# GpSimd instead of VectorE takes the remainder of every third weight block in a two-layer encoder

## The chip, the cores and the metric

One core of a Trainium2 chip runs the kernel. The metric is the device time of one execution in microseconds (us); the median of several runs is compared. Engines are named as in the profile: PE is TensorE (PEld its weight loads), DVE is VectorE, ACT is ScalarE, POOL is GpSimd, SP is the queue that issues most transfers.

## What is computed

A two-layer encoder on 256 tokens of 2048 numbers, all in float32:

```
x = x + neighbourhood_attention(rms_norm(x, na_norm))       # 16 heads of 128, learned bias
x = x + square(relu(rms_norm(x, ffn0_norm) @ ffn0_w1)) @ ffn0_w2     # 2048 -> 8192 -> 2048
x = x + dilated_attention(rms_norm(x, dil_norm))            # 3 groups of 8 heads
x = x + square(relu(rms_norm(x, ffn1_norm) @ ffn1_w1)) @ ffn1_w2
out = rms_norm(x, final_norm)
```

Nearly all of the work is products of the 256 tokens with weights. Each operand is cut into a rounded part and what is left of it, and a product is the sum of rounded x rounded, rounded x rest and rest x rounded.

## The kernel before

The weights are cut into 400 blocks of 512 x 512 numbers (1 MB), and the program is a list of 400 steps, one for each block; block i is used in step i. In the neighbourhood attention, steps 0 to 47, each of four groups of heads has twelve steps: four for q, four for k, four for v. Steps 48 to 63 are its output projection, then come feed-forward 0 (64 to 191), the dilated attention (192 to 271) and feed-forward 1 (272 to 399).

A step has four quarters of products on PE. Between them stand the small tasks of attention (scores, transposes, outputs). Nothing is scheduled by a tool: each engine takes its instructions in the order in which the loop at the end of the program writes them.

A block passes four hands. SP loads it into the tile w (three buffers). ACT then writes the rounded part wh of one half of the block (line 104), and DVE writes the rest, wl = w - wh (line 105); PE reads both. Each half has tiles of its own, and there are four buffers of wh and of wl, so two blocks' worth. In step i the first half of block i + 2 is cut behind quarter 1, the second half behind quarter 3; only then is block i + 5 loaded (lines 745 to 760), into the buffer of w that block i + 2 leaves. A half is named here (block, half), so (24, second) is the second half of block 24.

Two more things stand in these queues around the change. For each group of heads SP loads a bias, two transfers behind each of the steps 12c + 4 to 12c + 7 and thus behind the loads of the blocks 12c + 9 to 12c + 12 (`load_bias`, line 332; c is 0 to 3). DVE masks it after step 12c + 8 (`mask_bias`, line 338), adds it to the scores (line 368), takes the maximum (line 404), waits for ACT's exponentials (line 407) and scales (line 411). In the last step of q and of k, ACT copies half of the sums (line 144), DVE adds the other half (z, line 146) and scales z (line 348).

Of the kernel before, what the change touches and what calls it, by code (L numbers as in the profile page):

```python
# [8 lines left out]
F32 = mybir.dt.float32  # L9
F32R = mybir.dt.float32r  # L10
AF = mybir.ActivationFunctionType
ALU = mybir.AluOpType
AX = mybir.AxisListType

P = 128
# [11 lines left out]


class Step:
    """One weight block [4 x 128, 512], the products that it takes part in (in four  # L30
    quarters) and the work that goes with them: tasks have a part on the tensor engine
    after a quarter, evac reads the finished sums, post follows."""

    def __init__(self, src, quarters):
        self.src = src
# [7 lines left out]
def tile_encoder(ctx: ExitStack, tc: tile.TileContext, ins, out):  # L43
    nc = tc.nc
# [13 lines left out]
    x = const.tile([P, 2, D], F32, name="x")  # L58
# [9 lines left out]

    x_in = ins["x"].rearrange("(t p) d -> p t d", p=P)

# [1 line left out]
    steps = []  # L72

    def load(i):
# [11 lines left out]
    def prep(i, u):  # L86
        if i >= len(steps):
            return
        s = steps[i]
        hi = hlpool.tile([P, 2, 512], F32R, name="wh", tag="wh")  # L90
        lo = hlpool.tile([P, 2, 512], F32R, name="wl", tag="wl")
        part = s.w[:, 2 * u:2 * u + 2, :]
        if i:
            split(hi, lo, part)
        else:
            for a in range(2):
                split(hi[:, a], lo[:, a], part[:, a])
        s.hi[u], s.lo[u] = hi, lo
# [6 lines left out]
        nc.vector.tensor_tensor(out=dst_lo, in0=src, in1=dst_hi.bitcast(F32), op=ALU.subtract)  # L105

    def three(o, left, right, start, stop):
        """o += left.T @ right, both in two parts; the product of the two rests is below float32."""
        nc.tensor.matmul(o, left[0], right[0], start=start, stop=False)  # L109
        nc.tensor.matmul(o, left[0], right[1], start=False, stop=False)  # L110
        nc.tensor.matmul(o, left[1], right[0], start=False, stop=stop)  # L111

# [1 line left out]
    def gemm_cols(w, col, xT, nk, done):  # L114
        acc = {}
        made = []
# [39 lines left out]
        nc.tensor.matmul(o, xh, wl, start=False, stop=False)  # L156
        nc.tensor.matmul(o, xl, wh, start=False, stop=stop)  # L157

# [1 line left out]
    def gemm_rows(w, col, xT, ks, acc, first_k, last_k, apart=False):  # L160
        made = []
        for k in ks:
# [10 lines left out]
            made.append(s)  # L173
        return made

# [1 line left out]
    class Norm:  # L177
        def __init__(self, n, perm):
            self.n, self.perm = n, perm
# [68 lines left out]
            nc.vector.tensor_copy(self.r, self.r_ps[:, 0, 0:4].rearrange("p (t u) -> p t u", u=2)[:, :, 0])  # L248

    def rsqrt_mean(ss):  # L250
        """1 / sqrt(mean + eps) of the sums of squares: a root, its reciprocal and one step of Newton's on it."""
        a = small.tile([P, 2], F32, name="ms", tag="ms", bufs=2)
        nc.vector.tensor_reduce(out=a, in_=ss, op=ALU.add, axis=AX.X)
        nc.vector.tensor_scalar(out=a, in0=a, scalar1=1.0 / D, scalar2=EPS, op0=ALU.mult, op1=ALU.add)
        r = small.tile([P, 2], F32, name="rstd", tag="rstd", bufs=2)
        nc.scalar.sqrt(r, a)
        nc.vector.reciprocal(r, r)
        u = small.tile([P, 2], F32, name="ru", tag="ru", bufs=2)
        nc.vector.tensor_tensor(out=u, in0=r, in1=r, op=ALU.mult)
        nc.vector.tensor_tensor(out=u, in0=u, in1=a, op=ALU.mult)  # L260
        nc.vector.tensor_scalar(out=u, in0=u, scalar1=-0.5, scalar2=1.5, op0=ALU.mult, op1=ALU.add)
        nc.vector.tensor_tensor(out=r, in0=r, in1=u, op=ALU.mult)
        return r

    # x += rows; at the end of a sublayer the next norm is begun
    def add_rows(made, col_block, acc, norm, chunk_done):
        cs = slice(col_block * 512, (col_block + 1) * 512)
        if norm is not None and norm() in fin and col_block == NB - 1:
# [19 lines left out]
        later.append((i, pe, post, quarter))  # L288

    def pending_norm(get):  # L290
        """Hooks behind the steps that finish x's column blocks."""
        def chunk_done(step, c):
            i = steps.index(step)
            for half in range(2):
                at(i + 1, lambda half=half: get().transposes(c, half), lambda half=half: get().parts(c, half),
                   quarter=1 + half)
            if c == NB - 1:
                at(i, None, lambda: get().rstd())
                at(i + 2, lambda: get().rows(), lambda: get().rows_out())
                if get().perm:  # L300
                    at(i + 3, lambda: get().cols(), lambda: get().cols_out())
        return chunk_done

# [1 line left out]
    norms = [Norm(0, False), None, None, None]  # L305

    n0 = norms[0]
# [11 lines left out]
        return hi, lo  # L319

    class NaHeads:
        """Four heads: their q, k, v, bias and the steps from scores to outputs."""

        def __init__(self, c):
            self.c = c

        # bias[c + 64 e, h, o, 63 - c'] is for the query (2 t + e, c) and the key (o - 2 + 2 t, c')
        def load_bias(self, h):
            if h == 0:
                self.bias = big.tile([P, 4, 6, GRID_W], F32, name="bias", tag="big")  # L330
# [68 lines left out]
            split(t[:, h, 0, :], t[:, h, 1, :], self.o[:, 0, :])  # L399

    def softmax(p):
        """p [P, 2, n]: each row of n becomes its softmax."""
        m = small.tile([P, 2], F32, name="m", tag="m")
        nc.vector.tensor_reduce(out=m, in_=p, op=ALU.max, axis=AX.X, negate=True)
        z = small.tile([P, 2], F32, name="sum", tag="sum")
        for tb in range(2):
            nc.scalar.activation(p[:, tb, :], p[:, tb, :], AF.Exp, bias=m[:, tb:tb + 1],
                                 accum_out=z[:, tb:tb + 1])
        nc.vector.reciprocal(z, z)
        for tb in range(2):  # L410
            nc.vector.tensor_scalar(out=p[:, tb, :], in0=p[:, tb, :], scalar1=z[:, tb:tb + 1], scalar2=None,
                                    op0=ALU.mult)
# [4 lines left out]
    for c in range(4):  # L417
# [5 lines left out]
        i = steps.index(made[0])  # L423
# [5 lines left out]
        i = steps.index(made[0])  # L429
# [3 lines left out]
               lambda H=H, h=h, task=task: getattr(H, task + "_post")(h))  # L433

    def rows_apart(pair, xT, acc, finish):
        """The last two blocks of a sum of four: the first half of the tokens through both, then the second."""
        for tb, s in enumerate(pair):
            def quarter(s, n, tb=tb):
                for a in (n % 2 * 2, n % 2 * 2 + 1):
                    products(acc[tb], pair[n // 2], xT[2 + n // 2], a, slice(tb * P, (tb + 1) * P),  # L440
                             False, n == 3 and a == 3)
            s.quarters = quarter
            s.evac.append(lambda tb=tb: finish(tb, acc))
# [16 lines left out]
    out_rows(ins["na_wo"], na_oT, 4, lambda: norms[1], begin_norm(1, False),  # L460
             [(c, k) for c in range(3) for k in range(3)] + [(c, 3) for c in range(3)] + [(3, k) for k in range(4)])

# [1 line left out]
    def ffn(norm, w1, w2, next_norm, next_done):  # L464
        for g in range(4):
            hT = [None] * 4
# [14 lines left out]

    ffn(norms[1], ins["ffn0_w1"], ins["ffn0_w2"], lambda: norms[2], begin_norm(2, True))

# [1 line left out]
    n2 = norms[2]  # L485
    dil_oT = [None] * 2
    rope = {}
# [142 lines left out]
    out_rows(ins["dil_wo"], dil_oT, 2, lambda: norms[3], begin_norm(3, False),  # L630
             [(0, 0), (1, 0), (0, 1), (1, 1), (2, 0), (2, 1), (3, 0), (3, 1)])

# [1 line left out]
    class Final:  # L634
        perm = False

# [30 lines left out]
        def finish(self, tb, acc):  # L667
            cs = slice((NB - 1) * 512, D)
            nc.vector.tensor_tensor(out=x[:, tb, cs], in0=x[:, tb, cs], in1=acc[tb], op=ALU.add)
            self.square(NB - 1, tb)  # L670
            ms = small.tile([P, 1], F32, name="fms", tag="fms", bufs=2)
            nc.vector.tensor_scalar(out=ms, in0=self.ss[:, tb, NB - 1:], scalar1=1.0 / D,
                                    scalar2=self.part[:, tb:tb + 1], op0=ALU.mult, op1=ALU.add)
            # -2 / sqrt(ms): a root, its reciprocal and one step of Newton's on it; the gain has the factor -1/2
            r = small.tile([P, 1], F32, name="fr", tag="fr", bufs=2)
            nc.scalar.sqrt(r, ms)
            nc.vector.reciprocal(r, r)
            u = small.tile([P, 1], F32, name="fu", tag="fu", bufs=2)
            nc.vector.scalar_tensor_tensor(out=u, in0=r, scalar=ms, in1=r, op0=ALU.mult, op1=ALU.mult)
            nc.vector.scalar_tensor_tensor(out=r, in0=u, scalar=-3.0, in1=r, op0=ALU.add, op1=ALU.mult)  # L680
            for c in range(NB):
                cs = slice(c * 512, (c + 1) * 512)
                if c == 0:
                    nc.vector.tensor_scalar(out=x[:, tb, cs], in0=x[:, tb, cs], scalar1=r, scalar2=None,
                                            op0=ALU.mult)
                elif c == NB - 1:
                    nc.vector.scalar_tensor_tensor(out=x[:, tb, cs], in0=x[:, tb, cs], scalar=r, in1=self.g[:, cs],
                                                   op0=ALU.mult, op1=ALU.mult)
                else:
                    nc.scalar.activation(x[:, tb, cs], x[:, tb, cs], AF.Copy, scale=r)  # L690
                nc.sync.dma_start(self.o_v[:, tb, cs], x[:, tb, cs])
# [3 lines left out]
    at(len(steps) + 104, None, fin[0].halve)  # L695
    ffn(norms[3], ins["ffn1_w1"], ins["ffn1_w2"], lambda: fin[0], None)

# [1 line left out]
    for i, pe, post, q in later:  # L699
        if pe is None:  # L700
            steps[i].post.append(post)
# [129 lines left out]
```

## Time and profile before

| | us |
|---|---|
| median of 3 runs (2322.45 to 2324.16) | 2322.57 |
| profiled execution, its span | 2320.3 |
| PE busy | 2300.7 |
| DVE busy | 1406.0 |
| ACT busy | 1092.6 |
| POOL busy | 0.7 |

The profiled execution is one more execution; of it the profile gives the span, from the first instruction's start to the last one's end, and no time of its own. The median of the runs is 2.3 us above this span. Engines work side by side, so busy times do not add up; an engine that is busy for nearly all of the span sets its length. Matmuls overlap one another, so a busy PE is not PE at its peak.

### The profile page before, as it was taken

Reading aid. Unit: us, or ns where it says so; the run is one execution under the profiler, and the core shown is the slowest. Engines: PE = TensorE matmul, PEld = TensorE weight load, DVE = VectorE, ACT = ScalarE, POOL = GpSimd, SP = SyncE. Lnnn points to the kernel's source line nnn. Section 1 sums busy time; section 2 is a strip of 40 time slices with the busy share of each in tenths; the row PEclk is TensorE's granted clock in tenths of the full one; section 3 lists DMA queues with packets and bytes.
Section 4 is the critical chain, followed back from the end, with each engine's and each line's share of the span. In section 5 each row is a group of like instructions: output and inputs, shape, how many; then the busy total and the mean of one; then the engine's idle time right before and its main releaser. Section 6 shows DMA issues by size and latency. Waiting matters only on the chain.

```text
span 2320.3 us, 29178 instructions
## 1 busy us (share of the span) xinstructions
PE 2300.7 (99%) x11956; PEld 1963.1 (85%) x11956; DVE 1406.0 (61%) x1635; ACT 1092.6 (47%) x1390; POOL 0.7 (0%) x6
## 2 busy tenths in 40 slices
PE   8999999999999999999999999999999999999998
PEld 7888888888888888888888888888888888888886
DVE  6666765654555555566777667756654654555654
ACT  6444545543443453455444544445543543543443
POOL 0000000000000000000000000000000000000000
PEclk9999999999999999999999999999999999999999
DMA  7555655555555555555555545454555555555553
GB/s 248 169 175 176 191 182 170 182 197 200 182 187 194 185 196 189 193 181 188 189 179 184 177 164 181 164 181 169 191 192 193 182 200 187 189 187 200 200 192 135
DMA packets 73862, 430.36 MB, mean 185 GB/s; under 512 B 19776, under 2 KB 20352, under 8 KB 22528
## 3 DMA queue, kind: packets, MB, share of 16 engines
q1 hardware_dynamic: 73056, 426.80, 54.3%
q8 instruction: 93, 1.52, 0.3%
q10 hardware_dynamic: 672, 1.70, 0.2%
q14 instruction: 41, 0.34, 0.0%
HBM read 426.38 MB, written 2.10 MB: 185 GB/s over the span
## 4 chain that ended last, share of the span: by engine, by line
PE 98%; DMA 1%; DVE 1%; ACT 0%; issue 0%; SPq 0%; ACTq 0%; DVEq 0%
PE acc L134 33%; PE acc L136 17%; PE acc L156 15%; PE acc L155 15%; PE acc L157 15%; PE misc L194 1%; DMA bias<-in_rpb_dram 0%; PE misc L111 0%; PE misc L110 0%; PE misc L109 0%; DVE wl L105 0%; PE misc L593 0%; PE misc L553 0%; PE misc L380 0%; ACT wh L104 0%
## 5 line engine op out<-in xcount | busy, mean ns | idle before, releaser
L105 DVE TENSOR_TENSOR wl<-w,wh 128x1024 fp32r<-128x1024 f32 (+1 forms) x802 | 972.8, 1221 | 735.8 <-ACT wh L104 733.6
L104 ACT CAST wh<-w 128x1024 fp32r<-128x1024 f32 (+1 forms) x802 | 834.9, 1049 | 936.9 <-PE acc L157 460.2
L134 PE MATMUL acc<-xT,wh 128*128 128x512 f32 x3328 | 1178.5, 399 | 0.9 <-ACT wh L104 0.9
L136 PE MATMUL acc<-xT,wl 128*128 128x256 f32 x3328 | 935.0, 281 | 2.3 <-DVE wl L105 2.3
L134 PEld LDWEIGHTS acc<-xT,wh 128*128 128x128 f32 x3328 | 626.4, 188 | 150.4 <-ACT wh L104 1.9
L136 PEld LDWEIGHTS acc<-xT,wl 128*128 128x128 f32 x3328 | 629.8, 189 | 3.7 <-DVE wl L105 3.2
L155 PE MATMUL acc<-wh,hT 128*128 128x512 f32 x1024 | 399.5, 390 | 0.0
L156 PE MATMUL acc<-wl,hT 128*128 128x512 f32 x1024 | 399.0, 390 | 0.0
L157 PE MATMUL acc<-wh,hT 128*128 128x512 f32 x1024 | 398.9, 390 | 0.0
L157 PEld LDWEIGHTS acc<-wh,hT 128*128 128x128 f32 x1024 | 192.3, 188 | 39.9
L155 PEld LDWEIGHTS acc<-wh,hT 128*128 128x128 f32 x1024 | 192.3, 188 | 39.7
L156 PEld LDWEIGHTS acc<-wl,hT 128*128 128x128 f32 x1024 | 192.3, 188 | 39.4
L155 PE MATMUL acc<-wh,xT 128*128 128x512 f32 x320 | 126.7, 396 | 0.0
L156 PE MATMUL acc<-wl,xT 128*128 128x512 f32 x320 | 125.2, 391 | 1.1 <-DVE wl L105 1.1
L157 PE MATMUL acc<-wh,xT 128*128 128x512 f32 x320 | 124.9, 390 | 0.0
L144 ACT COPY b<-acc 128x512 f32<-128x512 f32 x104 | 60.7, 586 | 64.8 <-PE acc L136 59.1
L146 DVE TENSOR_TENSOR z<-acc,b 128x512 f32<-128x512 f32 x104 | 71.5, 691 | 25.8 <-ACT b L144 25.2
L155 PE MATMUL acc<-wh,oT 128*128 128x512 f32 x192 | 76.6, 399 | 0.0
L157 PE MATMUL acc<-wh,oT 128*128 128x512 f32 x192 | 75.0, 391 | 0.0
L156 PE MATMUL acc<-wl,oT 128*128 128x512 f32 x192 | 74.9, 390 | 0.0
L156 PEld LDWEIGHTS acc<-wl,xT 128*128 128x128 f32 x320 | 60.2, 188 | 13.1 <-DVE wl L105 1.8
L157 PEld LDWEIGHTS acc<-wh,xT 128*128 128x128 f32 x320 | 60.1, 188 | 12.5
(123 smaller groups left out, 1044.9 us busy)
## 6 DMA issues: line engine op xcount, KB each, us to landing
w<-in_ffn_w_dram SPq DMA_DIRECT2D x256, 1024.0 KB, 4.8
w<-in_dil_wqkv_dram SPq DMA_DIRECT2D x72, 1024.0 KB, 4.8
w<-in_na_wqkv_dram SPq DMA_DIRECT2D x47, 1024.0 KB, 4.9
w<-in_na_wo_dram SPq DMA_DIRECT2D x16, 1024.0 KB, 4.9
w<-in_dil_wo_dram SPq DMA_DIRECT2D x8, 1024.0 KB, 4.8
bias<-in_rpb_dram SPq DMA_DIRECT2D x32, 96.0 KB, 8.7
out_dram<-x SPq DMA_DIRECT2D x8, 256.0 KB, 2.5
x<-in_x_dram SPq DMA_DIRECT2D x3, 512.0 KB, 7.8
```

Source lines behind the costliest of these rows:

```text
L104: nc.scalar.copy(dst_hi, src)
L105: nc.vector.tensor_tensor(out=dst_lo, in0=src, in1=dst_hi.bitcast(F32), op=ALU.subtract)
L134: nc.tensor.matmul(o, s.hi[a // 2][:, a % 2, cs], xt.rearrange("p h t -> p (h t)"), start=first, stop=False)
L136: nc.tensor.matmul(o[:, :T], s.lo[a // 2][:, a % 2, cs], xt[:, 0, :], start=False, stop=last)
L144: nc.scalar.copy(b, acc[j][:, :, T:])
L146: nc.vector.tensor_tensor(out=z, in0=acc[j][:, :, :T], in1=b, op=ALU.add)
L155: nc.tensor.matmul(o, xh, wh, start=start, stop=False)
L156: nc.tensor.matmul(o, xh, wl, start=False, stop=False)
L157: nc.tensor.matmul(o, xl, wh, start=False, stop=stop)
L194: nc.tensor.transpose(self.tp[:, a, tb * P:(tb + 1) * P], x[:, tb, kt * P:(kt + 1) * P], ident)
```

## The change

In every third block from block 6 on (6, 9, ..., 399: 132 blocks, 264 halves) the subtraction of line 105 is issued on GpSimd. ACT's rounding stays where it was, and so do the tiles, the loads and the products. The other lines of the difference are comments and blank lines that keep the count.

```diff
@@ prep(i, u) @@
         part = s.w[:, 2 * u:2 * u + 2, :]
-        if i:
+        if i > 4 and i % 3 == 0:
+            nc.scalar.copy(hi, part)
+            nc.gpsimd.tensor_tensor(out=lo, in0=part, in1=hi.bitcast(F32), op=ALU.subtract)
+        elif i:
             split(hi, lo, part)
         else:
```

The first place is DVE's queue between the softmax of the first and of the second head in the first group (steps 9 to 11). Before, wl_717 is (11, second), wl_742 and wl_769 are the two halves of block 12, wl_792 is (13, first); p_693 and p_745 are the two heads' scores:

```order
L411 TENSOR_SCALAR p_693<-p_693,sum_698 128x256 x2
L105 TENSOR_TENSOR wl_717<-w_570,wh_716 128x1024
L105 TENSOR_TENSOR wl_742<-w_624,wh_741 128x1024
L368 TENSOR_TENSOR p_745<-misc_734,bias_483 128x256 x2
L404 TENSOR_REDUCE m_748<-p_745 128x2
L409 RECIPROCAL sum_750<-sum_750 128x2
L411 TENSOR_SCALAR p_745<-p_745,sum_750 128x256 x2
L105 TENSOR_TENSOR wl_769<-w_624,wh_768 128x1024
L105 TENSOR_TENSOR wl_792<-w_667,wh_791 128x1024
```

And the same stretch of DVE's queue with the change, where every line number is 3 higher:

```order
L414 TENSOR_SCALAR p_693<-p_693,sum_698 128x256 x2
L108 TENSOR_TENSOR wl_717<-w_570,wh_716 128x1024
L371 TENSOR_TENSOR p_745<-misc_734,bias_483 128x256 x2
L407 TENSOR_REDUCE m_748<-p_745 128x2
L412 RECIPROCAL sum_750<-sum_750 128x2
L414 TENSOR_SCALAR p_745<-p_745,sum_750 128x256 x2
L108 TENSOR_TENSOR wl_792<-w_667,wh_791 128x1024
```

Both halves of block 12 have left DVE: one subtraction fewer stands ahead of the second head's scores, and one fewer behind its scaling. On POOL's queue, empty before at this point, they stand behind those of the blocks 6 and 9, with what each waits for (the first half of a block among other things for its load):

```order
L95 TENSOR_TENSOR wl_457<-w_288,wh_456 128x1024 [waits DVE_49,DMAHW0_49,PE_49,Activation_49]
L95 TENSOR_TENSOR wl_478<-w_288,wh_477 128x1024 [waits DVE_49,PE_49,Activation_49]
L95 TENSOR_TENSOR wl_591<-w_481,wh_590 128x1024 [waits DMAHW3_49,PE_49,Activation_49]
L95 TENSOR_TENSOR wl_621<-w_481,wh_620 128x1024 [waits PE_49,Activation_49]
L95 TENSOR_TENSOR wl_742<-w_624,wh_741 128x1024 [waits DVE_49,DMAHW4_49,Activation_49,Pool_49]
L95 TENSOR_TENSOR wl_769<-w_624,wh_768 128x1024 [waits DVE_49,Activation_49,Pool_49]
```

POOL takes the halves in the order of the blocks and has nothing else to do between them. The second place is SP's queue, where the load of block 12 stands ahead of the last two transfers of the first group's bias. Before:

```order
L332 DMA bias<-in_rpb_dram 64x6x64
L332 DMA bias<-in_rpb_dram 64x6x64 [waits DMAHW3_49]
L81 DMA w<-in_na_wqkv_dram 128x2048 [waits DMAHW4_49,DVE_49]
L332 DMA bias<-in_rpb_dram 64x6x64 [waits DMAHW5_49]
L332 DMA bias<-in_rpb_dram 64x6x64 [waits DMAHW6_49]
```

With the change:

```order
L335 DMA bias<-in_rpb_dram 64x6x64
L335 DMA bias<-in_rpb_dram 64x6x64 [waits DMAHW3_49]
L81 DMA w<-in_na_wqkv_dram 128x2048 [waits DMAHW4_49,Pool_49]
L335 DMA bias<-in_rpb_dram 64x6x64 [waits DMAHW5_49]
L335 DMA bias<-in_rpb_dram 64x6x64 [waits DMAHW6_49]
```

The order is the same, but this load, and the bias behind it, now wait for POOL, since it overwrites the buffer of block 9. It is so in all four groups.

## Rows read from the trace of the kernel before

**Rows 1.** Page, part 1: busy time, share of the span and instructions of each engine.
```profile
PE 2300.7 (99%) x11956; PEld 1963.1 (85%) x11956; DVE 1406.0 (61%) x1635; ACT 1092.6 (47%) x1390; POOL 0.7 (0%) x6
```

**Rows 2.** Busy time by stretch, neighbourhood attention: stretch, length, engines, granted clock, DMA, GB/s.
```profile
50.00:340.00 290.00, 285.27 (x1542) 244.12 (x1541) 195.96 (x270) 141.57 (x221) 0.00 (x0) 1.00 0.57 178
```

**Rows 3.** Timeline, PE at step 12: start, length, [idle before, who ended it].
```profile
85.03 0.50 PE L134 MATMUL acc<-xT,wh 128*128 128x512 f32 x1 [0.35 <-ACT wh L104]
86.29 0.39 PE L136 MATMUL acc<-xT,wl 128*128 128x256 f32 x1 [0.76 <-DVE wl L105]
```

**Rows 4.** Timelines of DVE and ACT ahead of step 12.
```profile
79.17 2.36 DVE L105 TENSOR_TENSOR wl<-w,wh 128x1024 fp32r<-128x1024 f32 x2
81.44 0.75 DVE L368 TENSOR_TENSOR p<-misc,bias 128x256 f32<-128x256 f32 x2
85.01 2.36 DVE L105 TENSOR_TENSOR wl<-w,wh 128x1024 fp32r<-128x1024 f32 x2
...
83.95 1.98 ACT L104 CAST wh<-w 128x1024 fp32r<-128x1024 f32 x2
```

**Rows 5.** Groups by shape: count, busy us, mean ns of one, idle before.
```profile
L105 DVE TENSOR_TENSOR wl<-w,wh 128x1024 fp32r<-128x1024 f32 x798 | 970.2, 1223 | 735.8 <-ACT wh L104 733.6
...
masks.py:199 POOL TENSOR_SCALAR_AFFINE_SELECT ident<-ident 128x128 f32<-128x128 f32 x1 | 0.3, 292 | 0.1
```

**Rows 6.** Timelines of ACT and DVE around the end of step 19.
```profile
135.39 1.05 ACT L104 CAST wh<-w 128x1024 fp32r<-128x1024 f32 x1
...
134.83 1.39 DVE L146 TENSOR_TENSOR z<-acc,b 128x512 f32<-128x512 f32 x2 [0.39 <-ACT b L144]
136.47 1.23 DVE L105 TENSOR_TENSOR wl<-w,wh 128x1024 fp32r<-128x1024 f32 x1 [0.26 <-ACT wh L104]
137.62 1.29 DVE L348 SCALAR_TENSOR_TENSOR z<-z,rbc 128x512 f32<-128x512 f32 x2
...
148.93 1.76 DVE L338 TENSOR_TENSOR bias<-bias,namask 128x1536 f32<-128x1536 f32 x1 [5.41 <-DMA bias<-in_rpb_dram]
```

**Rows 7.** Transfers issued at 59.9, 137.7, 213.8, 289.8, 156.5 us: KB, us to landing.
```profile
w<-in_na_wqkv_dram SPq DMA_DIRECT2D x1, 1024.0 KB, 9.7
...
w<-in_na_wqkv_dram SPq DMA_DIRECT2D x1, 1024.0 KB, 5.7
...
w<-in_na_wqkv_dram SPq DMA_DIRECT2D x1, 1024.0 KB, 5.5
...
w<-in_na_wo_dram SPq DMA_DIRECT2D x1, 1024.0 KB, 5.6
...
w<-in_na_wqkv_dram SPq DMA_DIRECT2D x1, 1024.0 KB, 4.8
```

**Rows 8.** Timelines, (47, second): its subtraction (first of two), its first use.
```profile
307.20 2.36 DVE L105 TENSOR_TENSOR wl<-w,wh 128x1024 fp32r<-128x1024 f32 x2
...
308.80 0.39 PE L156 MATMUL acc<-wl,xT 128*128 128x512 f32 x1
```

**Rows 9.** Timelines, (222, second) and (399, second), each with its first use.
```profile
1295.28 2.36 DVE L105 TENSOR_TENSOR wl<-w,wh 128x1024 fp32r<-128x1024 f32 x2
...
1297.89 0.39 PE L156 MATMUL acc<-wl,xT 128*128 128x512 f32 x1
...
2301.55 1.23 DVE L105 TENSOR_TENSOR wl<-w,wh 128x1024 fp32r<-128x1024 f32 x1 [1.45 <-ACT wh L104]
...
2304.57 0.39 PE L156 MATMUL acc<-wl,hT 128*128 128x512 f32 x1
```

**Rows 10.** Timelines, (150, second) and (223, second), each with its first use.
```profile
880.73 1.22 DVE L105 TENSOR_TENSOR wl<-w,wh 128x1024 fp32r<-128x1024 f32 x1 [1.49 <-ACT wh L104]
...
887.83 0.39 PE L156 MATMUL acc<-wl,hT 128*128 128x512 f32 x1
...
1301.81 2.35 DVE L105 TENSOR_TENSOR wl<-w,wh 128x1024 fp32r<-128x1024 f32 x2
...
1304.22 0.40 PE L156 MATMUL acc<-wl,xT 128*128 128x512 f32 x1
```

## The prediction, written before the changed kernel ran

> **What bounds the kernel now.** I read the page's busy shares first: PE is busy 2300.7 us of the 2320.3 us span, DVE 61%, POOL 0.7 us in all [rows 1]. A change on DVE can therefore pay only where PE waits for DVE, so next I looked for PE's idle time by stretch. The neighbourhood attention holds 290.00 - 285.27 = 4.7 us of it [rows 2]. The rest lies before the first input has landed, and behind the last product, where no weight block is left to cut. In between PE never stops, at a granted clock of 1.00, the 2.4 GHz level, in the attention stretch and with no idle row after it. So the whole prize is 4.7 us, 0.2% of the time. I take a difference under 0.2% (4.6 us) as one that a measurement of this kernel can't tell from none.
>
> Where do the 4.7 us come from? PE's timeline shows that most are at one place which recurs three times, in the steps 12, 24 and 36, each the first of the next group's q. The reader is to see PE stop twice in step 12: 0.35 us for the rounded part of (12, second), then 0.76 us for its rest, 1.1 us together [rows 3]. Steps 24 and 36 look the same within 0.2 us. All three numbers divide by three, so the very subtractions that PE waits for go to GpSimd. What makes them late is upstream. DVE stands still for the bias (5.41 us before its masking in the second group [rows 6]); then come mask, scores, maximum, exponentials, and in ACT's and DVE's queues the cuts of the blocks stand between them [rows 4]. All that hangs on the landing of the bias.
>
> **The change, part by part.**
>
> *What leaves DVE.* 264 subtractions of 1.223 us [rows 5], 323 us of busy time. Nearly everywhere this is worth nothing: (150, second) is ready at 880.73 + 1.22 = 881.95 and first used at 887.83, 5.9 us later [rows 10]. I paired all 264 moved halves with their first use in this way, from (6, first) to (399, second): 240 have more than 4 us. The cover is the two blocks' worth of buffers. The relief counts at the three waits alone. There, (12, first) stands ahead of the second head's scores. The two subtractions take 2.36 us from 79.17, and the scores start at 81.44 [rows 4]; without the second one they start 2.36 - 1.22 = 1.14 us earlier, and so do the maximum, the exponentials, and ACT's rounding of (12, second), which began at 83.95 [rows 4].
>
> *What POOL costs.* No row shows a subtraction on POOL. The bounds: below, DVE's own 1.22 us. The nearest POOL row is the selection for the identity, 128 x 128 in 292 ns, one operand read and one written, 0.1 us behind its predecessor [rows 5]. Eight times the length makes 2.34 us; twice that, if two operands are read one after the other, makes 4.67 us, the upper bound. I take 2.34 us plus 0.1 us of hand-over, since it is the only row of this engine with a real tile, and its fixed part, counted eight times, makes up for some of a second operand. On DVE, rounding's end to rest's end is 135.39 + 1.05 = 136.44 to 137.70, or 1.26 us [rows 6]. So each moved half is ready x = 2.44 - 1.26 = 1.18 us later after its rounding.
>
> *At the three waits.* The rounding comes 1.14 us earlier and the rest takes 1.18 us longer: +0.04 us each. PE's first stop (0.35) goes, the second grows by the same. POOL has finished (12, first) by then: it starts when the rounding ends, about 80.1, or when DVE is done at 80.4.
>
> *The load behind it.* This is the term the difference doesn't show. SP loads block 12c + 12 only when (12c + 9, second) is cut, and the last bias transfers of the group are queued behind that load. In the second group, POOL could begin at 136.44 + 0.1 = 136.54. But DVE, free of its subtraction, goes straight to scaling z, which is complete at 134.83 + 1.39 = 136.22; the first of the two takes until 136.87 [rows 6]. I assume POOL waits for that one, 0.33 us. So load and bias are issued 1.18 + 0.33 = 1.5 us later. Some of it is absorbed, since the queue is still full: these four loads land 9.7, 5.7, 5.5 and 5.6 us after issue, against 4.8 us for one issued into an empty queue [rows 7], so they stood 4.9, 0.9, 0.7 and 0.8 us behind others. The bias, and all that hangs on it, is then later by 0, 0.6, 0.8 and 0.7 us in the four groups. In the fourth PE has not waited; its nearest use, (47, second), is ready at 307.20 + 1.22 = 308.42 and used at 308.80 [rows 8]: 0.4 us of margin, 0.3 us left.
>
> *The sum.* 3 x 0.04 + 0 + 0.6 + 0.8 + 0.3 = 1.8 us. On the profiled span that is 2322.1 us; with the 2.3 us by which the median stands above the span, 2324.4 us.
>
> *Elsewhere.* Every other load is also issued some 1.2 to 1.5 us later in every third step. It is hidden: a block lands 4.8 us after its issue [rows 7], and its first half is rounded only in the third step after, each step taking 2320.3 / 400 = 5.8 us on average. The tightest moved halves outside the attention of layer 0 are (222, second) and its twin (258, second) in the second attention, 1297.89 - 1296.50 = 1.4 us, and (399, second), 2304.57 - 2302.78 = 1.8 us [rows 9]. Each has more than x. If x grows beyond that, each costs the difference.
>
> **The rivals.**
>
> *Slower: the subtraction on POOL is dearer.* As a function of x the sum above is (x - 1.14) in the first group, 2x - 1.71 and 2x - 1.51 in the next two, x - 0.85 in the fourth: 6x - 5.2. That is 4.6 us at x = 1.63, a subtraction of 2.8 us. At the upper bound of 4.67 us, x is 3.51: 15.9 us there, 2 x 2.1 at (222, second) and its twin, 1.7 us at (399, second), 21.8 us in all: 2344.4 us. For it: the two operands. Against: half a price is no surprise for one fixed part counted eight times.
>
> *Slower: POOL and DVE take turns.* If an instruction that reads two operands from SBUF on DVE and one on POOL can't run together, each waits for the other's end. Then POOL may find both scalings of z ahead of it, 0.65 us more in three groups, +1.95 us. A DVE subtraction that meets POOL waits up to 2.34 us, which costs PE something where its own margin is smaller: (223, second), ready at 1303.03 and used at 1304.22 [rows 10], and its twin in the other half of the heads, up to 1.15 us each. 1.8 + 1.95 + 2.3 = 6.1 us: 2328.7 us. Against: in an average step of 5.8 us two halves are cut, 2.9 us apart, and a POOL subtraction of 2.34 us fits between; even wholly in turn the two engines have room, since DVE is busy for 61% [rows 1]. The row shows POOL idle, so nothing in this trace decides it. The Trainium skill has this rule: "SBUF — State Buffer", section "Who interferes with whom", says that a VectorE instruction with two SBUF inputs contends with a GpSimd instruction that reads SBUF, and that the one that comes second blocks until the first is done. By it the sum would be the 6.1 us of this rival at worst; without it, with POOL not even waiting for the first scaling of z, 0.8 us.
>
> *Faster: the waits go.* If POOL were as quick as DVE (1.22 us + 0.1), the three chains would end 1.08 us earlier and the load 0.4 us later, which the queue absorbs. PE gains 3 x 1.08 = 3.2 us: 2319.3 us, still within 0.2%. For more than 4.6 us every stop of this stage would have to go, also those before step 12 that wait for the bias and not for a cut.
>
> **How the numbers follow.** My forecast and its neighbourhood (subtraction of 1.9 to 2.8 us, little taking of turns): 62%, 2321.5 to 2327. A quicker POOL, 2319.3 to 2321.5: 8%, also within 0.2%. Dearer POOL: 16%, 2327 to 2344. Taking turns so that it shows: 10%, 2327 to 2330. Faster by over 0.2%: 4%. So faster 0.04, same 0.70, slower 0.26. The range 2320 to 2334 leaves out the lowest few per cent, about 6, and the dearer half of the dear subtractions, about 8.
>
> **What would show it.** 264 subtractions on POOL of about 2.3 us, each starting about 0.1 us after ACT's rounding. In steps 12, 24 and 36, PE without its stop for wh and a longer one for wl, 1.1 to 2 us together. The bias mask in groups two and three 0.6 to 0.8 us later relative to the step. DVE's busy time near 1406 - 323 = 1083 us, with no gain from it. Wrong I would be if POOL's subtraction takes over 2.8 us, if DVE's own subtractions are stretched or start late beside POOL's, or if PE stops anywhere after the first attention.

## The result and the profile after

With the change the median is 2328.52 us (13 runs, 2326.18 to 2329.8) against 2323.78 us for the kernel before (13 runs, 2321.76 to 2324.96): the ratio is 1.0021, 95% interval 1.0013 to 1.0029. It is slower by 4.7 us, at the edge of what was called no difference, inside the range, and in the direction of the forecast, but 2.9 us more than its sum. The likeliest class, "same", was given 0.70 and "slower" 0.26; the measured ratio falls just on the slower side of 0.2%, with an interval that lies on both sides of it. The time is above the band that the forecast gave to its own mechanism (2321.5 to 2327) and inside those of the two slower rivals, though neither of them turned out to be the cause. The kernel before is 1.2 us slower here than in the three runs that the forecast started from, so a part of this is the level of the runs.

The page of the changed kernel, span 2325.0 us: first the busy times [rows 1], then the groups of the two kinds of subtraction [rows 5].

```profile
PE 2301.6 (99%) x11956; PEld 1963.0 (84%) x11956; DVE 1186.7 (51%) x1371; ACT 1091.7 (47%) x1390; POOL 645.7 (28%) x270
...
L108 DVE TENSOR_TENSOR wl<-w,wh 128x1024 fp32r<-128x1024 f32 (+1 forms) x538 | 688.5, 1289 | 850.9 <-ACT wh L107 849.8
L95 POOL TENSOR_TENSOR wl<-w,wh 128x1024 fp32r<-128x1024 f32 x264 | 645.0, 2448 | 1662.5 <-ACT wh L94 1617.0
```

PE has the same work in the same busy time, 2301.6 us. 264 subtractions have gone to POOL at 2.45 us each; the ones that stayed on DVE have become longer on average, 1289 ns for 1223.

Where the 4.7 us arose can be read from the first product of a step. The timeline of PE, first the kernel before and then the changed one, at the start of step 8, step 50 and step 398:

```profile
56.98 0.39 PE L155 MATMUL acc<-wh,xT 128*128 128x512 f32 x1
323.68 0.39 PE L155 MATMUL acc<-wh,oT 128*128 128x512 f32 x1
2300.27 0.39 PE L155 MATMUL acc<-wh,hT 128*128 128x512 f32 x1
```
```profile
57.23 0.39 PE L158 MATMUL acc<-wh,xT 128*128 128x512 f32 x1
328.34 0.39 PE L158 MATMUL acc<-wh,oT 128*128 128x512 f32 x1
2304.96 0.39 PE L158 MATMUL acc<-wh,hT 128*128 128x512 f32 x1
```

The distance between the two kernels is 0.25 us at step 8, 4.66 us at step 50 and 4.69 us at step 398. The first 0.25 us were there at step 1 already, before any moved block. The other 4.4 us come from the neighbourhood attention; the 348 steps after that, with 88% of the moved halves, cost 0.03 us. Read off in the same way at the steps around 12, 24, 36 and 48, the four groups cost 0.9, 1.8, 0.7 and 1.0 us.

Within this stage, the busy times by stretch [rows 2] and PE's stops for a cut [rows 3], the seven that are longer than 0.2 us:

```profile
50.00:340.00 290.00, 281.56 (x1520) 240.21 (x1519) 178.87 (x234) 138.08 (x215) 72.30 (x30) 1.00 0.56 177
```
```profile
76.78 0.51 PE L159 MATMUL acc<-wl,xT 128*128 128x512 f32 x1 [1.34 <-DVE wl L108]
81.49 0.50 PE L159 MATMUL acc<-wl,xT 128*128 128x512 f32 x1 [0.56 <-DVE wl L108]
87.44 0.39 PE L139 MATMUL acc<-xT,wl 128*128 128x256 f32 x1 [1.53 <-POOL wl L95]
159.50 0.50 PE L159 MATMUL acc<-wl,xT 128*128 128x512 f32 x1 [0.57 <-DVE wl L108]
165.45 0.39 PE L139 MATMUL acc<-xT,wl 128*128 128x256 f32 x1 [1.51 <-POOL wl L95]
242.11 0.39 PE L139 MATMUL acc<-xT,wl 128*128 128x256 f32 x1 [1.52 <-POOL wl L95]
313.31 0.51 PE L159 MATMUL acc<-wl,xT 128*128 128x512 f32 x1 [0.56 <-DVE wl L108]
```

The largest rows name POOL, and it would be easy to stop there. But the stops at 159.50 and 313.31 are new and wait for subtractions on DVE, and the masking of the bias shows why. DVE's and POOL's timeline, first the first group's mask, then the second group's stretch around the end of step 19 [rows 6]:

```profile
73.83 1.76 DVE L341 TENSOR_TENSOR bias<-bias,namask 128x1536 f32<-128x1536 f32 x1 [7.68 <-DMA w<-in_na_wqkv_dram]
...
136.09 1.41 DVE L149 TENSOR_TENSOR z<-acc,b 128x512 f32<-128x512 f32 x2 [1.03 <-ACT b L147]
137.42 3.49 DVE L351 SCALAR_TENSOR_TENSOR z<-z,rbc 128x512 f32<-128x512 f32 x2
...
151.84 1.76 DVE L341 TENSOR_TENSOR bias<-bias,namask 128x1536 f32<-128x1536 f32 x1 [6.61 <-issue]
...
137.85 2.50 POOL L95 TENSOR_TENSOR wl<-w,wh 128x1024 fp32r<-128x1024 f32 x1 [1.46 <-ACT wh L94]
```

The first mask starts at 73.83, in the trace before at 72.79. The second starts at 151.84 instead of 148.93, 2.9 us later, while PE was only 1.24 us behind there. The wait is for the bias to land: the rows name a load of w, or nothing, but the mask reads no weights, and the last of the eight bias transfers landed 0.2 us before it, at 73.6 and 151.7 us. And the two scalings of z take 3.49 us instead of 1.29: DVE and POOL did take turns.

### The profile page after: what moved, and what is told of

Read it like the earlier page. It is cut to its first block, busy times and chain, and to the rows that moved or that the text cites. A ratio compares the mean times of both kernels' runs of the same rounds, so it can differ in the third digit from the quotient of the medians.

```text
span 2325.0 us, 29419 instructions
## 1 busy us (share of the span) xinstructions
PE 2301.6 (99%) x11956; PEld 1963.0 (84%) x11956; DVE 1186.7 (51%) x1371; ACT 1091.7 (47%) x1390; POOL 645.7 (28%) x270
## 4 chain that ended last, share of the span: by engine, by line
PE 95%; issue 1%; DMA 1%; DVE 1%; ACT 1%; POOL 1%; SPq 0%; ACTq 0%; DVEq 0%; POOLq 0%
PE acc L137 33%; PE acc L139 17%; PE acc L158 14%; PE acc L160 14%; PE acc L159 14%; DMA bias<-in_rpb_dram 1%; POOL wl L95 1%; PE misc L197 1%; PE misc L114 0%; PE misc L113 0%; PE misc L112 0%; DVE wl L108 0%; DMA w<-in_na_wqkv_dram 0%; PE misc L596 0%; PE misc L556 0%
## 5 line engine op out<-in xcount | busy, mean ns | idle before, releaser
L108 DVE TENSOR_TENSOR wl<-w,wh 128x1024 fp32r<-128x1024 f32 (+1 forms) x538 | 688.5, 1289 | 850.9 <-ACT wh L107 849.8
L95 POOL TENSOR_TENSOR wl<-w,wh 128x1024 fp32r<-128x1024 f32 x264 | 645.0, 2448 | 1662.5 <-ACT wh L94 1617.0
L107 ACT CAST wh<-w 128x1024 fp32r<-128x1024 f32 (+1 forms) x538 | 559.1, 1047 | 627.0 <-PE acc L160 305.0
L94 ACT CAST wh<-w 128x1024 fp32r<-128x1024 f32 x264 | 276.5, 1051 | 300.0 <-PE acc L160 151.5
```

What stands on the lines that cost most here:

```text
L94: nc.scalar.copy(hi, part)
L95: nc.gpsimd.tensor_tensor(out=lo, in0=part, in1=hi.bitcast(F32), op=ALU.subtract)
L107: nc.scalar.copy(dst_hi, src)
```

## The experiments

Two theories. A: the loss is the bias that lands late, because loads that wait for GpSimd stand ahead of it in SP's queue. B: the loss is GpSimd's price at the subtractions that PE waits for, and its taking turns with VectorE. Each run but two was timed several times beside the kernel before.

**GpSimd only after the first attention.**

```diff
-        if i > 4 and i % 3 == 0:
+        if i > 63 and i % 3 == 0:
```

> GpSimd subtracts every third block from block 66 on, 224 of the 264 halves; none in the neighbourhood attention. Theory A (all of the loss comes from the bias that lands later in that stage, since loads wait for GpSimd): no loss, within 0.5 us of the kernel before in the steps, span near 2320; PE's idle time in 50 to 340 us back from 8.4 to 4.7 us. Theory B (the loss comes from GpSimd's price and from taking turns with VectorE, wherever they meet): part of the 4.7 us stays after step 64, where 224 of the 264 halves are. VectorE's two-operand instructions in the feed-forward should be stretched as in the changed kernel by both theories; only B expects them to cost.

Measured: ratio 1.0002, interval 0.9993 to 1.0011. The 224 halves after step 63 cost nothing that can be told. That speaks against B as a general cost, but not yet against B at the three waits. PE's idle time in the stage came back from 8.4 to 5.65 us in its profile, not to the 4.7 expected: the first mask stood 0.8 us later relative to the steps although no load was late.

**The loads on time, one, the other, both.** In the first 48 blocks some stay on VectorE; the runs differ in the remainder that is left out:

```diff
-        if i > 4 and i % 3 == 0:
+        if i > 4 and i % 3 == 0 and not (i < 48 and i % 12 == 6):         # load of 12c + 9 on time
+        if i > 4 and i % 3 == 0 and not (i < 48 and i % 12 == 9):         # load of 12c + 12 on time
+        if i > 4 and i % 3 == 0 and not (i < 48 and i % 12 in (6, 9)):    # both
```

> As the changed kernel, but the blocks 6, 18, 30 and 42 stay on VectorE, so that the loads of the blocks 12c + 9 are issued on time, and only those of 12c + 12 late. Theory A (both late loads push back the transfer queue, and the bias with it): the loss falls from 4.7 us to about 1.8 us, the sum of the prediction, in which the queue absorbs the first 4.9, 0.9, 0.7 and 0.8 us; the wait in step 11 is back at about 0.55 us from 1.34. Theory A' (only the load of block 12c + 12 counts): unchanged, 4.4 us or more.

> As the changed kernel, but the blocks 9, 21, 33 and 45 stay on VectorE, so that the loads of 12c + 12, ahead of the last bias transfers, are issued on time, and those of 12c + 9 late. Theory A: a loss of 1 to 2.5 us stays, since the queue is full from the load of block 12c + 9 on and what is issued late there is late at its end too. Theory A': about 0.4 us, the price at steps 12, 24 and 36 alone.

> As the changed kernel, but the blocks 12c + 6 and 12c + 9 of the first 48 stay on VectorE; 12c and 12c + 3 stay on GpSimd. Theory A: the bias lands as before, and what is left is the price at steps 12, 24 and 36, about 0.1 us each: 0.2 to 0.6 us in all, no difference that the times can tell. Theory B: most of the 4.7 us stays, since the subtractions that TensorE waits for are on GpSimd still.

Measured: 1.0012 (1.0003 to 1.0021), or 2.5 us, with the load of 12c + 9 on time; 1.0035 (1.0022 to 1.0047), 7.4 us, with that of 12c + 12 on time; 1.0001 (0.9993 to 1.0010) with both. The last decides against B: the subtractions that PE waits for are on GpSimd in this run, and its stops there show it, in PE's timeline of that run:

```profile
85.92 0.38 PE L139 MATMUL acc<-xT,wl 128*128 128x256 f32 x1 [1.46 <-POOL wl L95]
162.13 0.38 PE L139 MATMUL acc<-xT,wl 128*128 128x256 f32 x1 [1.45 <-POOL wl L95]
238.31 0.39 PE L139 MATMUL acc<-xT,wl 128*128 128x256 f32 x1 [1.49 <-POOL wl L95]
```

Each is one stop of about 1.45 us by its row, where the kernel before had two, of 0.35 and 0.76 [rows 3]; and the time is the same. A stop that names an engine is not the price of that engine. The middle run was a surprise: one late load fewer, and dearer than the change as a whole. I had expected 1 to 2.5 us.

**One kind of block alone.** GpSimd takes only four blocks, so that nothing else differs:

```diff
-        if i > 4 and i % 3 == 0:
+        if i in (6, 18, 30, 42):
+        if i in (9, 21, 33, 45):
+        if i in (12, 24, 36, 48):
```

> GpSimd subtracts the blocks 6, 18, 30 and 42 alone, eight halves, so that of all loads only those of the blocks 12c + 9 are late. If a load that is late ahead of all eight bias transfers is what pushes the bias back, 5 to 8 us slower, as when the load of block 12c + 12 was on time (+7.4); if that run's excess came from something else on GpSimd, 0 to 2 us.

> GpSimd subtracts the blocks 9, 21, 33 and 45 alone, so that only the loads of the blocks 12c + 12 are late, ahead of the last two bias transfers of a group. As with the load of block 12c + 9 on time (+2.5): 1.5 to 3.5 us slower. The sum of the prediction, without its term at the waits, says 1.7 us.

> GpSimd subtracts the blocks 12, 24, 36 and 48 alone, the ones that TensorE waits for. The bias is on time. If 1.14 us of relief on VectorE and the dearer subtraction cancel, as the prediction has it, 0 to 0.4 us slower. If the price of 2.54 us stands alone, without relief, 3 to 4 us slower.

Measured: 1.0031 (1.0019 to 1.0044), 7.2 us; 1.0012 (1.0004 to 1.0021), 2.4 us; 1.0002 (0.9994 to 1.0011), 0.5 us. So the surprise stands without the other blocks: eight subtractions cost 7.2 us. None of PE's stops in the stage of the first of these runs waits for GpSimd; they wait for DVE and ACT, and these for the bias. Two masks of this run, with the blocks 6, 18, 30 and 42, and PE's longest stop with two of the products behind it; the last row is the busy time of the stretch from 80 to 82 us [rows 2]:

```profile
75.94 1.76 DVE L341 TENSOR_TENSOR bias<-bias,namask 128x1536 f32<-128x1536 f32 x1 [10.51 <-DMA w<-in_na_wqkv_dram]
153.51 1.76 DVE L341 TENSOR_TENSOR bias<-bias,namask 128x1536 f32<-128x1536 f32 x1 [6.83 <-DMA bias<-in_rpb_dram]
...
78.88 0.50 PE L159 MATMUL acc<-wl,xT 128*128 128x512 f32 x1 [3.44 <-DVE wl L108]
80.46 0.63 PE L160 MATMUL acc<-wh,xT 128*128 128x512 f32 x1
80.89 0.63 PE L158 MATMUL acc<-wh,xT 128*128 128x512 f32 x1
...
80.00:82.00 2.00, 2.00 (x6) 1.58 (x5) 0.80 (x4) 1.75 (x5) 0.00 (x0) 0.50 0.00 0
```

Behind the stop of 3.44 us the granted clock is 0.50, the 1.2 GHz level, and until 82.6 us the products follow one another in 0.43 us instead of 0.23, some 1.6 us in all. The run with the load of 12c + 12 on time shows the same clock from 79 to 81 us. In the changed kernel, whose longest stop is 1.53 us, the clock stays at 1.00 in this stage. So a late bias can bring a slower clock with it.

Block 6 delays the load of block 9, and all bias transfers of the group are issued behind that load. SP's queue over the second group shows it, the kernel before first, the changed kernel behind it:

```profile
120.01 0.33 SPq L81 DMA_DIRECT2D w<-in_na_wqkv_dram  x1
124.78 0.33 SPq L81 DMA_DIRECT2D w<-in_na_wqkv_dram  x1
131.03 0.33 SPq L81 DMA_DIRECT2D w<-in_na_wqkv_dram  x1
137.73 0.33 SPq L81 DMA_DIRECT2D w<-in_na_wqkv_dram  x1
```
```profile
123.40 0.33 SPq L81 DMA_DIRECT2D w<-in_na_wqkv_dram  x1
126.22 0.33 SPq L81 DMA_DIRECT2D w<-in_na_wqkv_dram  x1
132.38 0.33 SPq L81 DMA_DIRECT2D w<-in_na_wqkv_dram  x1
140.38 0.33 SPq L81 DMA_DIRECT2D w<-in_na_wqkv_dram  x1
```

These are the loads of the blocks 21 to 24, two bias transfers behind each. Before, they are 4.8, 6.3 and 6.7 us apart; after, the first comes 3.4 us later (2.2 us relative to PE's steps), only 2.8 us ahead of the second. The queue starts late into the stretch in which it is full, and does not catch up: with block 6 and its like alone, the last bias transfer of a group lands 1.4 to 2.9 us later relative to the steps than in the kernel before.

**The bias ahead of the load.** The test from the other side: nothing is taken off GpSimd, but the bias transfers of a step are issued just before the load of that step.

```diff
-            at(i + h, None, lambda H=H, h=h: H.load_bias(h))
+            steps[i + h].evac.append(lambda H=H, h=h: H.load_bias(h))
```

Once in the changed kernel, once in the kernel before:

> The changed kernel with the bias transfers of a step written ahead of the load of that step instead of behind it, so that they wait for no subtraction. Theory A (the loss is the bias that lands late behind loads that wait for GpSimd): the loss goes, and with it most of TensorE's 4.7 us of waits in this stage that the kernel before has as well: span 2315.5 to 2317, 4 to 4.7 us under the kernel before, and no wait for a subtraction on GpSimd in steps 12, 24 and 36, since rounding there comes some 4 us earlier. The mask starts 9 to 11 us after the start of step 12c + 8, against 14 to 15.8 before and 15.5 to 19 with the change. Theory B (GpSimd's price at the waits): TensorE still waits 1.5 us for GpSimd in the steps 12, 24 and 36, and the kernel is 1 to 4 us slower than the next run.

> The kernel before with the same edit to the bias transfers, all subtractions on VectorE. Theory A: 4 to 4.7 us faster than the kernel before, and within 0.5 us of the run with GpSimd and the bias first: then moving the subtractions costs nothing once no transfer hangs on them. If this one stays at 2320, the bias was not what the 4.7 us of waits came from.

Measured: 2315.09 us, ratio 0.9971 (0.9960 to 0.9982), with GpSimd, and 2315.46 us, 0.9972 (0.9961 to 0.9982), without. Both beat both kernels, by 7.4 and 7.0 us against the kernel before, 2322.45 us beside them, and they are equal as far as the times can tell. Busy times by stretch, with GpSimd and then without:

```profile
50.00:340.00 290.00, 290.00 (x1576) 250.05 (x1575) 177.96 (x242) 145.01 (x224) 77.25 (x32) 1.00 0.57 181
```
```profile
50.00:340.00 290.00, 290.00 (x1577) 250.03 (x1576) 199.65 (x273) 145.95 (x225) 0.00 (x0) 1.00 0.59 182
```

PE is busy for all 290 us. All of its waits in this stage came from the bias, and moving the subtractions costs nothing once no transfer hangs on them. The gain is more than I expected, and more than the 4.7 us of idle time [rows 2] that I had called the whole prize.

**Two cheaper instructions in GpSimd's place.** To price a second operand, the rest is replaced by a copy of w, or by zeros:

```diff
-            nc.gpsimd.tensor_tensor(out=lo, in0=part, in1=hi.bitcast(F32), op=ALU.subtract)
+            nc.gpsimd.tensor_copy(lo, part)
+            nc.gpsimd.memset(lo.bitcast(F32), 0.0)
```

> GpSimd copies w to wl, one operand, where the changed kernel subtracts: the rests of these blocks are wrong numbers, so only its times are read. How much of 2.40 us is the second operand? If the price goes by operands read, 1.2 to 1.4 us; if it goes by elements, 2.3 us, as the selection for the identity scaled up. At 1.3 us the loads are on time again and the attention stage loses nothing (1 us less than before, if the 1.14 us of relief is real). VectorE's instructions with two operands should still be stretched, by at most 1.3 us each, since the copy reads too.

> GpSimd fills wl with zeros where the changed kernel subtracts: the rests of these blocks are left out, so only its times are read. It still waits for ACT's buffers and for TensorE, and reads nothing. If VectorE is stretched because both read two operands through something that they share, its busy time falls from 1187 us to 1406 - 323 = 1083 us, and the second scaling of z in step 19 takes 0.65 us again instead of 2.8. If writes are enough, it stays stretched by the length of the fill.

Measured, one time each: 2315.99 and 2317.59 us, 5 to 6.5 us under the kernel before. Neither instruction waits for ACT's rounding, so the loads of 12c + 9 and 12c + 12 are issued 0.9 to 1.4 us earlier in their steps than in the kernel before, and that these two are faster says no more than that the loads matter. The groups of POOL, the copy first:

```profile
L95 POOL CAST wl<-w 128x1024 fp32r<-128x1024 f32 x264 | 299.6, 1136 | 1994.3 <-PE acc L139 1069.3 <-PE acc L159 844.9 <-DVE wl L108 37.6
```
```profile
L95 POOL MEMSET wl<- 128x1024 f32 x264 | 252.4, 956 | 2043.0 <-PE acc L139 1095.3 <-PE acc L159 892.6 <-DVE wl L108 37.8
```

No operand makes 0.96 us, one 1.14, a little under what was expected, and two make 2.45: a first operand adds 0.2 us at most, the second 1.3. That it is the operand, and not the operation, was not shown. DVE is busy for 1116.8 us beside the copy and 1093.7 us beside the fill, against 1186.7 us beside the subtraction and 1083 us by subtraction of the moved work. The 10 us beside the fill are no stretch: no group of DVE's instructions is longer there. Neighbours overlap in the records (two subtractions of 1.22 us take 2.36 [rows 4]), so one that goes takes less than its length off the busy time.

**All blocks.** The dose to the other end:

```diff
-        if i > 4 and i % 3 == 0:
+        if i > 4:
```

> GpSimd subtracts all blocks from 5 on, 790 halves of 2.54 us, 2007 us of GpSimd in 2320. If only loads that wait for it and the bias behind them cost, 3 to 10 us slower, since every half still fits between two (2.9 us apart). If taking turns with VectorE or GpSimd's capacity decides, it falls behind in the steps with many tasks and the loss is 20 us or more, with waits outside the first attention too.

Measured: 2330.32 us, 1.0030 (1.0018 to 1.0043), 7.9 us, within the first expectation; but the place is not the expected one. POOL's own group, 82% of the span:

```profile
L95 POOL TENSOR_TENSOR wl<-w,wh 128x1024 fp32r<-128x1024 f32 x790 | 1913.7, 2445 | 397.3 <-ACT wh L94 395.6
```

By PE's first products only 1.4 us of its profile's 8.3 us are there at step 50: 4.8 us arise up to step 12, and 3.7 come back at the steps 12, 24 and 36, where the stops of the kernel before are gone. Another 5.4 us arise between the steps 192 and 272, in the second attention, where the changed kernel loses nothing. Most of it, 3.1 us, lies in step 194. PE's stop there, one of DVE's instructions ahead of it, and the stretch behind it:

```profile
1138.43 0.61 PE L246 MATMUL misc<-ident,rbc 128*128 128x2 f32 x4 [1.39 <-DVE rbc L241]
...
1133.13 2.12 DVE L217 TENSOR_TENSOR xT<-gx,xT 128x256 fp32r<-128x256 f32 x1
...
1140.10:1143.10 3.00, 3.00 (x11) 2.52 (x11) 2.40 (x6) 0.00 (x0) 0.39 (x1) 0.50 0.57 240
```

PE waits for DVE here, not for GpSimd: four of these additions of the norm take 1.49 to 2.36 us beside GpSimd's subtractions, where each took 0.42 before. Behind the stop the granted clock is 0.50 again. So with all blocks moved, taking turns does cost time, as this trace reads; no run tested it apart. The expectation had the right size, but for a loss of another place and cause.

## Why the prediction was right, and where it was wrong

**What bounds the kernel** held: PE is busy as before, 323 us of relief on DVE bought nothing that can be told, and but for 0.25 us the difference arose in the one stage where PE had waited before, though not only at the places where it had: the stops at 159.50 and 313.31 are new. The claim that 4.7 us were the whole prize was wrong: removing those waits gave 7.0 to 7.4 us. An idle row counts from the modelled end of the last product, and that end is not where PE could have gone on. Of the two stops in step 12, 1.1 us by their rows [rows 3], the next product starts 85.03 to 86.29, 1.26 us, behind its forerunner, where such a pair stands 0.23 us apart at 56.63 and 56.86 in the same trace: 1.03 us lost there for a row of 0.76.

**What POOL costs** was right: 2.40 us in the median and 0.13 us of hand-over, for 2.34 and 0.1; x is 1.28 where I had 1.18. The way to it was luck. It took one operand's row eight times, 2.34 us, and let the fixed part stand for the second operand; measured, a copy with one operand takes 1.14 us, half of that, and the second operand 1.3 us more.

**At the three waits** +0.04 us each was right within what can be told: alone these blocks cost 0.5 us in the times, with an interval from -1.4 to +2.6 us, and by PE's first products nothing in their profile beyond step 8. ACT's rounding of (12, second) starts at 83.86 while everything is 1.04 us late, a relief of 1.1 us for the 1.14 of the sum.

**The load behind it** is the step that failed. It said that SP's load of block 12c + 12 waits for GpSimd and pushes the bias back, by 1.7 us of loss. This mechanism alone was measured at 2.4 us, and the term that was under-sized is the second group's. In the run with the blocks 9, 21, 33 and 45 the last bias transfer landed, relative to the steps, 0.4 us earlier than before in the first group, and 2.5, 0.7 and 0.9 us later in the others, for 0, 0.6, 0.8 and 0.7 in the sum. In the second group the load did land faster, 4.9 us after its issue for 5.7 [rows 7], but the bias behind it did not, 10.5 us for 10.0: the absorption was read from the load, and the mask waits for the bias. But the change makes a second load late, that of block 12c + 9, which overwrites the buffer of block 12c + 6 and stands ahead of all eight bias transfers; the sum had filed it under "every other load", hidden because a block lands long before it is used. The block is indeed early enough. What stands behind it in the queue is not: alone this load costs 7.2 us. And the absorption that I counted on for the first group, 4.9 us, was a queue that was full because its loads had come on time; with the load of block 9 late, the first group's mask came 1.04 us later rather than not at all (73.83 for 72.79), 0.8 of it beyond the 0.25 us by which PE was behind. That amount is not certain: in the run without GpSimd before block 66 the first mask stood 0.8 us later too, so it varies from run to run.

The two late loads together cost 4.7 us, less than the earlier one alone. The landing of a group's last bias transfer, counted from the first product of step 12c + 4, says where. The four groups, how much later it lands than in the kernel before (37.9, 38.8, 38.7 and 38.6 us), and what the group costs by PE's first products:

| | last bias transfer, us later | cost of the group, us |
|---|---|---|
| changed kernel | 0.8, 1.7, 0.5, 1.2 | 0.9, 1.8, 0.7, 1.0 |
| blocks 6, 18, 30, 42 alone | 2.9, 1.4, 2.1, 2.2 | 2.9, 1.4, 2.2, 2.0 |

Each group costs about what its bias is late. The slower clock in the first group of the second run adds nothing to this that can be told: the stops behind it are shorter, 1.1 us by their rows for 2.4 in the changed kernel. Why the last transfer lands later when the next load is on time is seen in part. In the run with block 6 and its like alone the bias transfers of the third head are caught by the next load, issued 3.0 us into step 8, and land 12.0 us into that step; in the changed kernel that load comes 1.4 us later and they land 10.4 us into it, though issued at the same place. In this case, then, a load that came later let the transfers ahead of it finish sooner. That this is the whole reason was not shown: in the second group the third head's transfers differ in the same way, and the last one lands 0.3 us earlier, not later, than in the changed kernel.

**The rivals.** A dearer subtraction did not come; 2.8 us would have been needed. Taking turns did come, as a fact: the two scalings of z at step 19 took 3.49 us, and no such pair did before. The Trainium skill's rule ("SBUF — State Buffer", section "Who interferes with whom") was right, down to its exemption of instructions that do not read: beside zeros written by GpSimd, DVE's scalings of z and its subtractions have their old mean of 683 and 1224 ns. I assumed POOL would wait for the first scaling; it was DVE's second one that waited, and POOL lost 0.1 us. The price that I had put on it, 4.3 us over the sum, did not come: with 224 of the 264 halves still on GpSimd there was no loss, and in the stage itself none with the bias on time. The 98 us by which DVE's instructions were stretched lie in its idle time. With all blocks on GpSimd they no longer did, as the second attention shows.

## What to carry to other kernels

When an instruction is moved to a slower engine, list who is released by its end, and not only who reads its result. Here the readers themselves lost nothing that could be told, and the loss came through the buffer that it frees: a load waits for it, and small transfers stand behind that load in the queue. A transfer that something waits for belongs ahead of the ones that wait for buffers; that one line was worth 7 us here, with either engine.

## What the runs showed of the hardware

GpSimd took 2.40 us in the median to subtract two tiles of 128 x 1024, VectorE 1.22; a copy took 1.04 in the median and a fill 0.95. A VectorE instruction with two operands in SBUF that meets a GpSimd instruction which reads waits for it and shows the wait as its own length: subtractions of 1.22 us ran up to 3.35 us, pairs of scalings 3.49 for 1.29. By the lengths of all its instructions the stretch was 98 us beside the subtraction, 24 beside a copy on GpSimd and 0.4 beside a fill. TensorE's granted clock fell to 0.50, the 1.2 GHz level, behind a stop of 3.44 us in the run with the blocks 6, 18, 30 and 42, and behind one of 1.39 us in the run with all blocks, but not behind the stops of the changed kernel, of 1.53 us at most; what decides it no run here shows.
